# Weights behind the attention: split by two GpSimd loads instead of a load, a cast and a subtraction

## The chip, the cores and the metric

The kernel runs on one core of a Trainium2 chip. The metric is the device time of one execution in microseconds. The profile is of one execution, taken by the hardware profiler.

## The reference

One layer of a hybrid decoder block over 512 real positions and 16 leading meta positions, 1024 wide, all in fp32. Two attention branches of 16 heads each run side by side (MLA with rotary parts, and FoX with a cumulative forget gate), and their outputs are merged:

```python
u = rmsnorm(h, pre_norm_g)
proj = u @ w_in                        # q, k, v, z of both branches, gate_a, gate_b
...
y_mla = (o_mla * silu(z_mla)) @ w_br_mla
y_fox = (o_fox * silu(z_fox)) @ w_br_fox
mixed = (sigmoid(gate_a) * y_mla + sigmoid(gate_b) * y_fox) @ w_out
h = h + rmsnorm(mixed, post_norm_g)    # the meta positions are dropped at the end
```

## The kernel before

**Products in three passes.** TensorE multiplies a rounded fp32 type (`F32R`). To keep fp32 accuracy each operand is cut in a high half, its rounded value, and a low half, the rounded rest. A product is then three: high by high, high by low, low by high. A projection of 1024 inputs, 128 outputs and 512 positions is a *unit* of 8 x 3 = 24 products, accumulated in one bank of PSUM (three banks, pool `accp`). A unit's `done` takes the bank up.

**Weights.** `wload` asks SyncE's queue for a raw block of 128 x 1024 fp32 (512 KB, in rows of 512 bytes for `w_in` and the branch weights, of 2 KB for `w_out`). `wsplit` makes its halves: ScalarE casts raw to `wh` (L130), then `split_lo` (L103) subtracts, `wl = raw - wh`. The engine of the subtraction is `low[0]`: GpSimd up to the end of the attention, VectorE behind it. Raw blocks and both halves lie in the pool `wp`, three rooms of 4 KB per partition for each of `wraw`, `wh` and `wl`. A unit's halves are made when its first product is placed in the program, and `weights(...).load` lets the raw load be asked for up to three units ahead.

**What stands behind the attention.** The order of TensorE is written out by hand (`manual_schedule`); the other engines' orders, and those of the queues, are made by a scheduler from when things are ready and their priorities. The attention is filled up with projections, among them five gate units (`pg`); its last one, `tail`, surrounds the last product of the attention with its values (`ov`). Then the pools of the attention's inputs (`fctx`, `cctx`) are closed, and there follow:

- `halved_g(1)`, which cuts the FoX branch's output `gT[1]` into `gh` and `gl` (ScalarE and VectorE), and eight units `py(i, 1)` with `w_br_fox`, a gate unit behind each of the first three;
- `halved_g(0)`, four gate units, and eight units `py(i, 0)` with `w_br_mla`, a gate unit behind each of the first four;
- the product with `w_out` in a Strassen-like form of seven products of 24 each. Six of the fourteen weight blocks are loaded (`plain`, two 512-wide rows of `w_out` to a block), and eight are sums or differences that VectorE makes ahead of time in `tb` (`summed`);
- the second norm, the residual and the output.

That makes 11 gate units and 16 `py` units behind the attention, and 6 `plain` blocks. `gh` and `gl` lie in a pool `m2` of 16 KB each that opens behind the attention, and `yo` and `xr` (16 KB each) and `gp` (4 KB) in a pool `o1` that opens when `m2` is closed.

Of the kernel before, what the change touches and what calls it, by code (L numbers as in the profile page):

```python
# [12 lines left out]
F32R = mybir.dt.float32r  # L13
# [4 lines left out]
ALU = mybir.AluOpType  # L18
# [9 lines left out]
KD = D // 128  # L28
# [7 lines left out]
O_CQ, O_ZM, O_FQ, O_FK, O_FV, O_F, O_ZF, O_GA, O_GB = 0, 416, 1440, 2464, 3488, 4512, 4528, 5552, 6576  # L36
# [13 lines left out]
def f32(ap):  # L50
    return ap.bitcast(F32)
# [3 lines left out]
def block_kernel(ctx: ExitStack, tc: tile.TileContext, x, meta_tokens, pre_norm_g, w_in, fox_forget_b,  # L55
                 mla_q_norm_g, mla_kv_norm_g, w_uq, w_ukv, w_br_mla, w_br_fox, w_out, post_norm_g,
                 rope_tok, rope_pe, out):
    nc = tc.nc
    x2 = x[0]
    out2 = out[0]  # L60
    win = w_in[0].rearrange("(k p) f -> p k f", p=128)
    wout = w_out[0].rearrange("(k p) f -> p k f", p=128)
    wbr = [w_br_mla[0].rearrange("(k p) f -> p k f", p=128), w_br_fox[0].rearrange("(k p) f -> p k f", p=128)]
# [16 lines left out]
    c_dram = dram.tile([2, NH, L], F32, tag="cdram", name="c_dram")  # L80
    qpe_dram = dram.tile([NH, 2, 2, 16, S], F32, tag="qpedram", name="qpe_dram")

    wp = ctx.enter_context(tc.tile_pool(name="wp", bufs=3))
    uid = [0]
    written, sums_out = [False], []
    behind, through, first_t, exps, halved, lowered = [], [], [], [], {}, {}
# [1 line left out]
    def dma(out, src, start=None):  # L88

        with tc.issue_after(sums_out[1]) if written[0] and len(sums_out) == 2 else nullcontext():  # L90
            ins = (start or nc.sync.dma_start)(out=out, in_=src)
        if written[0]:
            tc.keep_in_program_order(ins)
        return ins.ins

    def mm(*a, **k):
        nc.tensor.matmul(*a, **k)  # L97
# [4 lines left out]
    def split_lo(eng, lo, src, hi):  # L102
        return eng.tensor_tensor(out=lo, in0=src, in1=f32(hi), op=ALU.subtract)  # L103

    def wload(srcs):

        uid[0] += 1
        u = uid[0]
        raw = wp.tile([128, 1024], F32, tag="wraw", name=f"wraw{u}")
        n = 0  # L110
        parts = []
        for src in srcs:
            dims = src.shape[1:]
            w = int(np.prod(dims))
            names = "abcd"[: len(dims)]
            pat = f"p ({' '.join(names)}) -> p {' '.join(names)}"
            rv = raw[:, n : n + w].rearrange(pat, **{c: d for c, d in zip(names, dims)})
            dma(rv, src)
            parts.append((n, w))
            n += w  # L120
        return u, raw, parts, n

    low = [nc.gpsimd]

    def wsplit(ld):

        u, raw, parts, n = ld
        wh, wl = (wp.tile([128, 1024], F32R, tag=t, name=f"{t}{u}") for t in ("wh", "wl"))
        with tc.issue_after(behind[0]) if behind else nullcontext():
            nc.scalar.copy(wh[:, :n], raw[:, :n])  # L130
        split_lo(low[0], wl[:, :n], raw[:, :n], wh[:, :n])
        return [(wh[:, o : o + w], wl[:, o : o + w]) for o, w in parts]

    def wunit(srcs):
        return wsplit(wload(srcs))

    def weights(srcs, wrap):

        st = {}

        def load():
            if "l" not in st:
                st["l"] = wload(srcs())

        def get():
            load()
            return wrap(wsplit(st["l"]))
        get.load = load
        return get

    def by_k(part, nk):

        h, l = (t.rearrange("p (k f) -> p k f", k=nk) for t in part)
        return (lambda k: h[:, k, :]), (lambda k: l[:, k, :])
# [15 lines left out]
    def acc(name):  # L170
        return accp.tile([128, 512], F32, tag="acc", name=name)
# [3 lines left out]
    def unit(name, getw, act, nk, sls, done):  # L175

        st = {}
        out = []

        def prep():  # L180
            if "w" not in st:
                st["w"] = getw()
            return True
        for i, sl in enumerate(sls):
            n = sl.stop - sl.start
            for k in range(nk):
                def fn(i=i, sl=sl, k=k, n=n):
                    if "b" not in st:
                        st["b"] = prep()
                        for load in getattr(out[0][1], "nxt", ()):  # L190
                            load()
                    if k == 0:
                        st["ps"] = acc(f"{name}{i}")
                    ps = st["ps"][:, :n]
                    (wh, wl), (ah, al) = st["w"], act(k)
                    for q, (w, a) in enumerate(((wh, ah), (wh, al), (wl, ah))):
                        mm(ps, w(k), a[:, sl], start=(k == 0 and q == 0), stop=(k == nk - 1 and q == 2))
                    if k == nk - 1:
                        done(i, ps)
                out.append((3 * n / 2.4, fn))  # L200
        out[0][1].prep = prep
        if hasattr(getw, "load"):
            out[0][1].load = getw.load
        return out

    REAL = [slice(META, L)]
# [11 lines left out]
    def win_w(off, i):  # L218
        return weights(lambda: [win[:, :, off + 128 * i : off + 128 * i + 128]], lambda w: by_k(w[0], KD))

    def run(steps):
        for _, fn in steps:
            fn()
# [322 lines left out]
    def gate_unit():  # L546

        i, br = gates.pop(0)

        def done(_, ps):  # L550
            ths[i, br] = thp.tile([128, S], F32, tag="th", name=f"th{i}{br}")
            nc.scalar.activation(ths[i, br], ps, AF.Tanh, scale=0.5)
        return unit(f"pg{i}{br}", win_w((O_GA, O_GB)[br], i), u_act, KD, REAL, done)


    with ExitStack() as att:
# [299 lines left out]
        def feed(br, pr):  # L856

            q = (q_mla, q_fox)[br](pr)
            k = (k_mla, k_fox)[br](pr)
            v, vts[br, pr] = v_unit(br, pr)  # L860
            return q, k, v
# [13 lines left out]
        for si, (br, pr) in enumerate(stages):  # L875
            last = si + 1 == len(stages)
            if not last:
                q, k, v = feed(*stages[si + 1])
# [87 lines left out]

    fctx.close()
    cctx.close()
    low[0] = nc.vector
    with ExitStack() as mg:  # L970
        mg.enter_context(tc.manual_schedule(engines={mybir.EngineType.PE}))
# [16 lines left out]

        def py(i, br):
            def get():  # L990
                return by_k(wunit([wbr[br][:, :, 128 * i : 128 * i + 128]])[0], KD)

            def done(_, ps):
                nc.vector.scalar_tensor_tensor(out=gT[br][:, i], in0=ths[i, br], scalar=1.0, in1=ps, op0=ALU.add, op1=ALU.mult)
            run(unit(f"py{i}{br}", get, lambda k: (gh[:, k, :], gl[:, k, :]), KD, [slice(0, S)], done))
            if br:
                return
            nc.vector.tensor_tensor(out=mx[:, i], in0=mx[:, i], in1=gT[1][:, i], op=ALU.add)
            src, (h, l) = (mx[:, i, 0:256], [t[:, i] for t in a1]) if i < HK else (mx[:, i], [t[:, i - HK] for t in a2])
            nc.scalar.copy(h, src)  # L1000
            split_lo(nc.vector, l, src, h)
# [20 lines left out]
        for i in range(KD):  # L1022
# [3 lines left out]
            if i == 2:  # L1026
                for n, (kb, c) in enumerate(((0, 0), (0, 1), (1, 1), (1, 0))):
                    for half in range(2):
                        k0 = HK * kb + 2 * half
# [7 lines left out]
        for n, i in enumerate(PAIRED):  # L1037
# [3 lines left out]
            elif n >= 4:  # L1041
                done = n // 2 if n < 7 else HK
# [18 lines left out]

        def plain(kb, n, c):
            k0 = HK * kb + 2 * c
            return by_k(wunit([wout[:, k0 : k0 + 2, 512 * n : 512 * n + 512]])[0], 2)

        def summed(n, c):
            uid[0] += 1
# [126 lines left out]
```

## Time and profile before

| | |
|---|---|
| time, median of 3 runs | 604.22 us (604.12 to 605.11) |
| the profiled execution | 603.71 us, of which the profile's span 601.8 us |
| TensorE products | 592.5 us busy, 98% of the span |
| VectorE, ScalarE, GpSimd | 62%, 57%, 30% busy |
| granted TensorE clock | 0.998 of full |
| last product of the attention | ends at 407.7 us |
| last gate of the attention | ends at 410.7 us |
| last `py` unit | ends at 557.6 us |
| last product | ends at 596.0 us |

A name like `wl<-wraw,wh` in a row of the profile is the tile written and the tiles read, without buffer numbers. `L103` is line 103 of the kernel. A row marked `SPq` is an issue of SyncE's DMA queue. Busy time of an engine says nothing on the end by itself; what counts is the chain of waits.

### The profile page before, as it was taken

The page shows a single profiled execution, that of the slowest core. Times are in us where ns is not written, and L with a number is a line of the kernel's source. Part 1 is how long each engine was busy: PE and PEld are TensorE (multiplying, and loading weights), DVE is VectorE, ACT ScalarE, POOL GpSimd, SP SyncE. Part 2 cuts the span into 40 slices and gives each one's busy share as a digit, 9 for nine tenths or more (in the row PEclk, how much of TensorE's full clock was granted, in tenths as well). Part 3 has the DMA queues.
Part 4 walks back from the last instruction along what each step waited for, and adds up shares of the span by engine and source line. Part 5 has one row for each costly group of instructions (what it writes and reads, how often), then busy time and mean ns, then how long its engine had stood idle before and what let it go on. Part 6 is the DMA issues. An engine that isn't in the chain of part 4 may idle for free.

```text
span 601.8 us, 10999 instructions
## 1 busy us (share of the span) xinstructions
PE 592.5 (98%) x3777; PEld 501.7 (83%) x3777; DVE 374.1 (62%) x1002; ACT 343.9 (57%) x788; POOL 180.6 (30%) x239
## 2 busy tenths in 40 slices
PE   8999999999999999999999999999999999999996
PEld 6889779789889889888898898888888888888884
DVE  4956776674675674766657747764733524367857
ACT  7847765774783784766747747851222423353653
POOL 4316635443348453443523534430000000000000
PEclk9999999999999999999999999999999999999999
DMA  8433699899796798988886875988533333332603
GB/s 294 107 84 86 134 196 208 193 189 231 96 185 152 171 200 178 189 191 170 163 158 154 201 160 140 193 163 281 182 97 105 106 86 89 105 104 91 228 0 141
DMA packets 219960, 93.25 MB, mean 155 GB/s; under 512 B 133420, under 2 KB 211636, under 8 KB 219904
## 3 DMA queue, kind: packets, MB, share of 16 engines
q1 hardware_dynamic: 219904, 92.55, 65.5%
q8 instruction: 30, 0.49, 0.3%
q14 instruction: 26, 0.21, 0.1%
HBM read 58.10 MB, written 4.00 MB: 103 GB/s over the span
## 4 chain that ended last, share of the span: by engine, by line
PE 92%; ACT 3%; DMA 2%; DVE 1%; issue 1%; POOL 1%; SPq 0%; DVEq 0%; ACTq 0%; POOLq 0%
PE z L97 16%; PE py L97 14%; PE pg L97 14%; PE v L97 9%; PE st L97 8%; PE fq L97 8%; PE fk L97 7%; PE ov L97 5%; PE x L97 4%; PE psm L97 2%; PE mq L97 2%; PE mk L97 1%; PE ppe L97 1%; DMA wsr<-in_w_in_dram 1%; PE y L97 1%; DMA ht<-in_x_dram 1%
## 5 line engine op out<-in xcount | busy, mean ns | idle before, releaser
L103 POOL TENSOR_TENSOR wl<-wraw,wh 128x1024 fp32r<-128x1024 f32 (+2 forms) x63 | 122.6, 1954 | 105.3 <-ACT wh L130 76.5
L130 ACT CAST wh<-wraw 128x1024 fp32r<-128x1024 f32 (+1 forms) x80 | 83.1, 1042 | 115.7 <-PE pg L97 38.6
L823 DVE SCALAR_TENSOR_TENSOR pn<-sf,ri,pn 128x128 f16<-128x128 f32 (+3 forms) x128 | 70.7, 592 | 13.9 <-ACT pn L822 13.8
L795 ACT ACTIVATE sf<-sf,nb 128x144 f32<-128x144 f32 (+3 forms) x128 | 72.0, 564 | 8.1 <-DVE nb L787 7.8
L822 ACT ACTIVATE pn<-sf,ri 128x128 f16<-128x128 f32 (+3 forms) x128 | 61.5, 551 | 20.4 <-ACT sf L795 17.6
L103 DVE TENSOR_TENSOR wl<-wraw,wh 128x1024 fp32r<-128x1024 f32 x33 | 40.3, 1223 | 42.4 <-ACT wh L130 42.4
L787 DVE CUSTOM_DVE_ANT_0 sf<-st,maskt 128x272 f32<-128x272 f32 (+2 forms) x128 | 48.6, 435 | 3.9 <-PE st L97 3.9
L97 PE MATMUL z<-uTh,wh 128*128 128x512 f32 x128 | 50.9, 398 | 0.0
L97 PE MATMUL z<-uTh,wl 128*128 128x512 f32 x128 | 50.1, 392 | 0.3 <-POOL wl L103 0.3
L97 PE MATMUL pg<-uTh,wh 128*128 128x512 f32 x128 | 50.3, 393 | 0.0
L97 PE MATMUL z<-uTl,wh 128*128 128x512 f32 x128 | 50.0, 391 | 0.0
L97 PE MATMUL pg<-uTl,wh 128*128 128x512 f32 x128 | 49.8, 389 | 0.0
L97 PE MATMUL pg<-uTh,wl 128*128 128x512 f32 x128 | 49.8, 389 | 0.0
L97 PE MATMUL py<-gh,wh 128*128 128x512 f32 x128 | 49.8, 389 | 0.0
L97 PE MATMUL py<-gl,wh 128*128 128x512 f32 x128 | 49.8, 389 | 0.0
L97 PE MATMUL py<-gh,wl 128*128 128x512 f32 x128 | 49.8, 389 | 0.0
L97 PE MATMUL st<-hlk,hlq 64*128 64x272 f32 (+3 forms) x480 | 47.3, 306 | 0.0
L97 PEld LDWEIGHTS st<-hlk,hlq 64*128 64x128 f32 x480 | 35.0, 185 | 5.8 <-ACT vh L719 2.8
L700 DVE TENSOR_REDUCE vsc<-v 128x1 f32<-128x272 f32 (+1 forms) x32 | 13.2, 432 | 37.9 <-PE v L97 37.9
L97 PE MATMUL v<-uTh,wl 128*128 128x256 f32 (+1 forms) x128 | 36.5, 285 | 0.0
L97 PE MATMUL fk<-uTl,wh 128*128 128x256 f32 (+1 forms) x128 | 36.4, 285 | 0.0
L97 PE MATMUL fk<-uTh,wh 128*128 128x256 f32 (+1 forms) x128 | 36.4, 285 | 0.0
(233 smaller groups left out, 1431.4 us busy)
## 6 DMA issues: line engine op xcount, KB each, us to landing
wraw<-in_w_in_dram SPq DMA_DIRECT2D x56, 512.0 KB, 4.1
wraw<-in_w_br_fox_dram SPq DMA_DIRECT2D x8, 512.0 KB, 3.6
tb<-in_w_out_dram SPq DMA_DIRECT2D x8, 512.0 KB, 7.4
wraw<-in_w_br_mla_dram SPq DMA_DIRECT2D x8, 512.0 KB, 3.6
wraw<-in_w_out_dram SPq DMA_DIRECT2D x6, 512.0 KB
pt<-pn SPq DMA_TRANSPOSE x128, 3.1
xr<-in_x_dram SPq DMA_DIRECT2D x4, 512.0 KB, 7.4
out_dram<-yo SPq DMA_DIRECT2D x8, 256.0 KB, 2.0
```

Source lines behind the costliest of these rows:

```text
L97: nc.tensor.matmul(*a, **k)
L103: return eng.tensor_tensor(out=lo, in0=src, in1=f32(hi), op=ALU.subtract)
L130: nc.scalar.copy(wh[:, :n], raw[:, :n])
L700: nc.vector.tensor_reduce(out=sc[:, i : i + 1], in_=ps, op=ALU.max, axis=AX.X, apply_absolute_value=True)
L787: nc.vector.tensor_tensor_reduce(out=sf_of(h, b)[:, c0 : c0 + w], in0=ps[h][:, o : o + w], in1=maskt[:, m0 : m0 + w], scale=-scale, scalar ...
L795: exps[g] = nc.scalar.activation(sf, sf, AF.Exp, bias=sums["nb"][:, h, b : b + 1], scale=-1.0, accum_out=sums["su"][:, h, b : b + 1]).ins
L822: nc.scalar.activation(hi, sf, AF.Copy, scale=rib)
L823: nc.vector.scalar_tensor_tensor(out=lo, in0=sf, scalar=rib, in1=hi, op0=ALU.mult, op1=ALU.subtract)
```

## The change

Behind the attention the pool `wp` is closed and a pool `wq` opened, with four rooms of 8 KB per partition, each for both halves of a block. A block's halves are made by a new function, `wdma`, without a raw copy on the chip: GpSimd issues a load that casts from fp32 to the rounded type on its way into `wh`; ScalarE writes `wl = -wh`; GpSimd issues the same load a second time, adding into `wl`. The 11 gate units built behind the attention, the 16 `py` units and the 6 `plain` blocks use it. The eight `summed` blocks keep the cast and the subtraction on VectorE, and take their halves' room from `wq`. The gate units inside the attention keep `win_w`.

```diff
-    wp = ctx.enter_context(tc.tile_pool(name="wp", bufs=3))
+    wctx = ExitStack()
+    wp = wctx.enter_context(tc.tile_pool(name="wp", bufs=3))
+    wq = []
...
     def wsplit(ld):
 
         u, raw, parts, n = ld
-        wh, wl = (wp.tile([128, 1024], F32R, tag=t, name=f"{t}{u}") for t in ("wh", "wl"))
+        if wq:
+            both = wq[0].tile([128, 2, 1024], F32R, tag="w", name=f"w{u}")
+            wh, wl = both[:, 0], both[:, 1]
+        else:
+            wh, wl = (wp.tile([128, 1024], F32R, tag=t, name=f"{t}{u}") for t in ("wh", "wl"))
...
-    def wunit(srcs):
-        return wsplit(wload(srcs))
+    def wdma(src):
+
+        uid[0] += 1
+        u = uid[0]
+        both = wq[0].tile([128, 2, 1024], F32R, tag="w", name=f"w{u}")
+        wh, wl = both[:, 0], both[:, 1]
+        rv = [w.rearrange("p (k f) -> p k f", k=src.shape[1]) for w in (wh, wl)]
+        nc.gpsimd.dma_start(out=rv[0], in_=src)
+        nc.scalar.mul(wl, f32(wh), -1.0)
+        nc.gpsimd.dma_start(out=rv[1], in_=src, accum_op=ALU.add)
+        return wh, wl
...
-        return unit(f"pg{i}{br}", win_w((O_GA, O_GB)[br], i), u_act, KD, REAL, done)
+        off = (O_GA, O_GB)[br] + 128 * i
+        get = win_w(off - 128 * i, i) if low[0] is nc.gpsimd else lambda: by_k(wdma(win[:, :, off : off + 128]), KD)
+        return unit(f"pg{i}{br}", get, u_act, KD, REAL, done)
...
     fctx.close()
     cctx.close()
+    wctx.close()
+    wq.append(ctx.enter_context(tc.tile_pool(name="wq", bufs=4)))
     low[0] = nc.vector
...
-                return by_k(wunit([wbr[br][:, :, 128 * i : 128 * i + 128]])[0], KD)
+                return by_k(wdma(wbr[br][:, :, 128 * i : 128 * i + 128]), KD)
...
-            return by_k(wunit([wout[:, k0 : k0 + 2, 512 * n : 512 * n + 512]])[0], 2)
+            return by_k(wdma(wout[:, k0 : k0 + 2, 512 * n : 512 * n + 512]), 2)
```

## The prediction

> **What bounds the kernel now.** I read the busy time of the engines first, then the stretches behind the attention, then the chain of waits there. The windows view gives per row: the stretch, its length, then busy time and instructions of PE, its weight loads, VectorE (DVE), ScalarE (ACT) and GpSimd (POOL), the granted TensorE clock, the DMA engines' busy share and GB/s.
>
> ```profile
> PE 592.5 (98%) x3777; PEld 501.7 (83%) x3777; DVE 374.1 (62%) x1002; ACT 343.9 (57%) x788; POOL 180.6 (30%) x239
> 443.00:470.00 27.00, 27.00 (x121) 22.37 (x120) 11.66 (x14) 9.51 (x13) 0.00 (x0) 1.00 0.35 95
> 470.00:557.00 87.00, 87.00 (x386) 72.06 (x385) 42.18 (x58) 30.45 (x44) 0.00 (x0) 1.00 0.33 96
> 557.00:596.00 39.00, 38.93 (x171) 31.61 (x169) 31.10 (x49) 23.22 (x41) 0.00 (x0) 1.00 0.30 112
> ```
>
> TensorE is busy in the whole of every stretch behind the attention, at the full clock; VectorE is busy half of the middle one, ScalarE a third, GpSimd not at all. Work taken off VectorE there cannot shorten anything. The chain of waits, in order of time (start, length, what), says the same:
>
> ```profile
> 407.74 2.95 PE pg L97 x12
> 410.69 5.44 PE py L97 x24
> 416.13 5.44 PE pg L97 x24
> 421.57 5.44 PE py L97 x24
> ...
> 535.81 21.76 PE py L97 x96
> 557.57 5.44 PE x L97 x24
> ...
> 590.23 5.73 PE x L97 x24
> ```
>
> Each of the 27 units `pg` (11) and `py` (16) is 24 products in 5.44 us, so 0.227 us a product, and the next begins in the moment the last one ends. There is no gap to close, so the change can gain nothing here; the question is only whether the weights still arrive in time.
>
> Who brings them now is seen in the issues of SyncE's queue (start, length, what) in the page's list of DMA issues, whose last number is the median from issue to landing, and in the tile view of the raw weights (ns: shortest/median/longest, then the first and last start):
>
> ```profile
> 382.28 0.37 SPq L91 DMA_DIRECT2D wraw<-in_w_br_fox_dram  x1
> 387.75 10.86 SPq L91 DMA_TRANSPOSE pt<-pn  x8
> 408.56 1.40 SPq L1030 DMA_DIRECT2D tb<-in_w_out_dram  x3
> wraw<-in_w_in_dram SPq DMA_DIRECT2D x56, 512.0 KB, 4.1
> wraw<-in_w_br_fox_dram SPq DMA_DIRECT2D x8, 512.0 KB, 3.6
> tb<-in_w_out_dram SPq DMA_DIRECT2D x8, 512.0 KB, 7.4
> L103 DVE TENSOR_TENSOR wl<-wraw,wh x33: 1212/1224/1227, 399.6 to 577.5; 128x1024 fp32r<-128x1024 f32 x33
> L130 ACT CAST wh<-wraw x80: 637/1053/1129, 24.0 to 576.4; 128x1024 fp32r<-128x1024 f32 x78, 128x512 fp32r<-128x512 f32 x2
> ```
>
> The first `py` unit starts at 410.69, and its raw weights were asked for at 382.28, 28 us ahead and in the middle of the attention. A load, a cast of 1.05 us and a subtraction of 1.22 us are hidden many times over.
>
> **The change part by part.**
>
> *Taken away, at no gain.* For the 33 units with weights of their own (11 gates, 16 `py`, 6 `plain`) 33 subtractions on VectorE go (33 x 1.224 = 40 us) and 33 loads leave SyncE's queue. ScalarE keeps 33 passes of the same size, a negation in place of the cast; I take 1.05 us. All of that lay under 100% TensorE, so its removal is worth nothing. Nothing of the 11 gates' work inside the attention changes: the units built there still take the old way.
>
> *The transition.* The new rooms take the place of the old weight pool, which is closed before them; everything below it on that side was closed too. What a new pool waits for is shown once, at the end of the `py` units, where `yo`, `xr` and `gp` go where `gh` and `gl` were (SyncE's queue, the waits there, and the last row of GpSimd):
>
> ```profile
> 557.60 0.34 SPq L1057 DMA_DIRECT2D gp<-in_post_norm_g_dram  x1
> SPq L1057 <- PE py L97: 2.9, 1, 2.9
> 395.13 2.79 POOL L103 TENSOR_TENSOR wl<-wraw,wh 128x1024 fp32r<-128x1024 f32 x1
> ```
>
> `gp` is declared behind `yo` and `xr`, which alone fill the 32 KB of `gh` and `gl`, and yet its load sits in SyncE's queue for 2.9 us until the last `py` product (535.81 + 21.76 = 557.57). So the first use of a pool waits for the last use of all that lay in the pool beneath. The last user of the old weight pool is the gate `pg` that ends at 407.74 + 2.95 = 410.69. Before that no room of the new pool may be filled; GpSimd, whose last own instruction starts at 395.13, waits there with 66 loads behind it, and TensorE, whose order is written out, has nothing else to do. The old pool is 9 rooms of 4 KB, the new one 4 of 8 KB; the halves `gh` and `gl`, which come next, so move onto the old pool's last 4 KB and wait for the same moment; their first piece takes one ScalarE and one VectorE pass of some 0.7 us and the rest keeps pace, so the weights cover it.
>
> TensorE then stands still for casting load, negation, adding load. Neither kind of load is in this trace. From below each is bounded by the fastest load of 512 KB, 3.6 us; from above I use 7.4 us, the landing of loads of that size that were issued in a burst (`tb`). For the casting load I take 4.1 us (`w_in`, the same size and 512-byte rows). For the adding one I take 7.4 us: four rooms are free at once, so it stands behind three more casting loads. 4.1 + 1.05 + 7.4 = 12.55 us (ends: 8.25 and 15.85).
>
> By the formula of the Trainium skill (DMA: Bandwidth & Descriptors, "Anatomy of one DMA"), 2.0 us plus the bytes at 436 GB/s, a load issued by GpSimd would take an estimated 3.2 us; the gap would then be 7.5 us, the pace of the later units 5.6 us, and the whole about 614 us, near my lower end. No run here has such a load yet.
>
> *The clock after that gap.* TensorE idles at the start and at the end of this run:
>
> ```profile
> 2.07 4.34 PE L97 MATMUL spun<-CT,ONE 128*128 128x512 f32 x10 [2.07 <-DVE ONE L236]
> 596.00:599.00 3.00, 0.00 (x0) 0.00 (x0) 2.83 (x5) 0.97 (x3) 0.00 (x0) 1.00 0.45 175
> 599.00:602.00 3.00, 0.00 (x0) 0.00 (x0) 0.00 (x0) 0.00 (x0) 0.00 (x0) 0.65 0.45 175
> ```
>
> After the last product at 596.0 the clock stays full for 3 us and averages 0.65 in the next 3; if it falls to half, that is at about 599.9, 3.9 us into the idle time. The first ten products of the run took 0.434 us each, against 0.227 later. A gap of 12.55 us is long enough, so I add 10 x (0.434 - 0.227) = 2.1 us once (ends: 0 and 2.1). The Trainium skill has this as a rule (TensorE: Matmul & The Clock Gate, "What's actually happening"): half clock after about 3.4 us without work, full clock again after about 3.4 us of work, which would make it about 1.7 us; the trace's last two stretches agree with the first half of it.
>
> *The pace afterwards.* Of a unit the adding load must wait for the negation, and that for the casting load; both loads are issued by GpSimd in order. Where the queue alternates, casting and adding load of one unit, then of the next, the next unit's casting load stands behind this unit's adding load. Then one unit costs the casting load's landing, the negation, and the issue of the adding load. The issue is bounded by the two kinds in SyncE's queue: 0.37 us for a plain load, 10.86 / 8 = 1.36 us for a transposing one. I take 1.36, since these requests are the harder kind. 4.1 + 1.05 + 1.36 = 6.51 us against 5.44: 1.07 us a unit (ends: 0, since 3.6 + 1.05 + 0.37 = 5.02 is below 5.44; and 7.4 + 1.05 + 1.36 - 5.44 = 4.37).
>
> Four units have rooms at once, 23 follow. Each of those has a lead of three units, 16.32 us, against a chain of 12.55, so 3.8 us are free before the loss is felt: 23 x 1.07 - 3.8 = 20.8 us. Why alternating is likelier than not: in the present kernel a room comes free only when TensorE is done with it, one each 5.44 us, and a load with its negation (5.15 us) is done before the next comes free.
>
> *The output product.* Its first four weights are used up in 2.72 us each, half a unit. The last of their rooms comes free as the last `py` ends, TensorE arrives 3 x 2.72 = 8.2 us later, and its chain takes at least 4.1 + 1.05 + 4.1 = 9.25: 1.1 us lost (ends: 0 and 7.7). The eight `summed` weights come from a buffer that is there and stay as they are.
>
> *Sum*, on the profiled execution's own 603.71 us: 603.7 + 12.55 + 2.1 + 20.8 + 1.1 = 640.2 us. The median of the runs lies 0.5 us above the profiled one, so 640.7. The lower ends give 603.7 + 8.25 = 612, the upper ones 603.7 + 15.85 + 2.1 + 100 + 7.7 = 729 (the 100 is 23 x 4.37 less the half microsecond that is left of the lead).
>
> **The rivals.**
>
> *The transition alone.* If the order of GpSimd's queue has the next unit's casting load ahead of this unit's adding load, two chains overlap, a chain of 12.55 us fits into the lead of 16.32, and only the first gap, the clock and the output product stay: 603.7 + 12.55 + 2.1 + 1.1 + 0.5 = 620. For it: the order of the queues follows when things are ready and not the text (the `py` load at 382.28 stands ahead of transposes of the attention). Against it: the 5.15 us above. Chance 0.25.
>
> *The DMA engines become the bound.* Now a unit's one load keeps them busy 0.33 of the time, 0.33 x 5.44 = 1.8 us. An adding load must also read what it adds to. At three times a plain load for both together they would be busy 5.4 of 5.44 us, which is just hidden; at four times for the adding load alone it is 5 x 1.8 = 9.0 us a unit, 23 x 3.56 = 82 us, and the whole 603.7 + 12.55 + 2.1 + 82 + 1.1 + 0.5 = 702. It decides from 5.44 us on. For it: an adding load has to fetch twice what a casting one does, and no row here bounds its price from above. Against it: none shows an addition to be slow either. The Trainium skill (Collectives: The Full Stack, "The bandwidth ceiling") holds that an adding transfer is slower for its two reads and not for the addition; by that rule the pace would stay at 5.4 us and this rival would fall. Chance 0.13.
>
> *Not slower.* If the new rooms wait only for the tiles that lay where they are, the first ones, over raw buffers that have long been read, can be filled in the attention. It decides at 410.69 - 12.55 = 398.1: a first casting load issued before that leaves no gap, and with a hidden pace the time is 604. It can end below that by no more than the few tenths of noise, as TensorE has no idle time to give. Against it stands the wait of `gp`. Chance 0.05 for no change and 0.02 for faster.
>
> That the casting load copies the bits and does not round would make the low halves zero, and change no time: the number of products is the same.
>
> **How the numbers follow.** The forecast, a gap and an alternating queue, has 0.55; the rivals have 0.25, 0.13, 0.05 and 0.02. The range 612 to 729 takes in the ends of the forecast's terms, the whole of the second case, and the lighter half of the third; about 0.8. A measurement of this kernel tells about 0.2%, 1.2 us, from no change. Slower by more than that: 0.55 + 0.25 + 0.13 and a little of the fourth case, 0.94; same 0.04; faster 0.02.
>
> **What the changed profile would show.** Right: a gap of TensorE from 410.7 on that ends with an adding load, of 8 to 16 us; a lower clock just behind it; from then on short gaps ahead of each `pg` and `py` unit, some 1 us, put down to a DMA; GpSimd's queue waiting for ScalarE's negation with a casting load behind it; VectorE 40 us less busy, everything ahead of 405 us as before. Wrong: a first casting load before 398 (no gap); units at 5.44 us back to back behind the gap (first rival); DMA engines at a share near 1, or GpSimd busy without a break while TensorE waits (the bound lies in the loads themselves, and the pace is far above 6.5 us).

## The result and the profile after

The change makes the kernel slower: 696.88 us median (693.49 to 697.26, four runs) against 604.66 us (604.12 to 605.55, four runs), a ratio of 1.151 with a 95% interval of 1.147 to 1.155. The profiled execution took 696.67 us, with a span of 694.9 us; before it was 603.71 and 601.8.

The page of the changed kernel: busy time of the engines, the granted clock and the DMA engines' share in 40 slices, the engines' shares in the chain that ended last, and the loads with the median from issue to landing:

```profile
PE 619.4 (89%) x3777; PEld 515.9 (74%) x3777; DVE 334.5 (48%) x969; ACT 342.9 (49%) x788; POOL 256.7 (37%) x305
PEclk9999999999999999999999995899998998988789
DMA  9524798998869899598877649999999989997453
PE 56%; issue 21%; DMA 8%; POOL 8%; ACT 4%; DVE 1%; SPq 0%; DVEq 0%; POOLq 0%; ACTq 0%
w<-in_w_in_dram POOLq DMA_DIRECT2D x22, 512.0 KB, 7.6
w<-in_w_br_fox_dram POOLq DMA_DIRECT2D x16, 512.0 KB, 7.7
...
w<-in_w_out_dram POOLq DMA_DIRECT2D x12, 512.0 KB, 7.2
```

TensorE does the same 3777 products, but it carries 56% of the chain where it carried 92%. VectorE lost 39.6 us of work and the end of the kernel did not feel it. The clock, at full speed throughout before, falls in the 25th slice (417 to 434 us), just behind the attention, and shows less than nine tenths in seven of the fifteen slices after that. The new loads take 7.2 to 7.7 us to land, in the median of both kinds together.

Where the time went is seen in the windows behind the attention (columns as in the prediction):

```profile
412.60:442.00 29.40, 8.65 (x24) 6.47 (x25) 14.26 (x16) 8.94 (x13) 10.08 (x8) 0.59 1.32 277
442.00:500.00 58.00, 49.84 (x207) 39.92 (x206) 4.13 (x6) 8.77 (x10) 18.18 (x15) 0.95 0.91 137
500.00:560.00 60.00, 50.77 (x197) 39.95 (x196) 8.00 (x13) 14.95 (x22) 19.78 (x16) 0.90 0.98 142
560.00:628.00 68.00, 56.39 (x217) 44.76 (x217) 17.89 (x30) 18.98 (x29) 21.56 (x18) 0.87 0.89 139
628.00:670.00 42.00, 27.65 (x109) 21.50 (x108) 16.62 (x27) 17.34 (x28) 8.92 (x9) 0.86 0.69 169
```

TensorE's idle time is the length of a row less its busy time: 20.75 us in the first, then 8.16, 9.23 and 11.61, and 14.35 in the stretch of the output product. Of the 29.0 us in the three middle rows, 27 are seven waits of 2.5 to 5.2 us each, and not a short one ahead of each unit. Set against the profile before, the span of 694.9 us is made up as follows. All values are in us.

| part | before | after | more | forecast |
|---|---|---|---|---|
| to the end of the last gate | 410.7 | 412.5 | 1.9 | 0 |
| first gap | 0 | 20.8 | 20.8 | 12.55 |
| the other `pg` and `py` units: idle | 0 | 29.0 | 29.0 | } 20.8 pace |
| the same: slower products | 146.9 | 167.6 | 20.7 | } and 2.1 clock |
| output product | 38.4 | 59.0 | 20.5 | 1.1 |
| behind the last product | 5.8 | 6.0 | 0.2 | 0 |

The gate's end, the end of the last `py` unit at 629.9 and that of the last product at 688.9 are read from TensorE's timeline; 167.6 is what is left of 412.5 to 629.9 without the idle time.

The first gap, from the timelines of TensorE, GpSimd, ScalarE and SyncE's queue (start, length, what, and in brackets the idle time ahead with what ended it; L147 is the casting load, L148 the negation, L149 the adding load):

```profile
412.15 0.39 PE L99 MATMUL pg<-uTh,wl 128*128 128x512 f32 x1
410.48 4.32 SPq L1049 DMA_DIRECT2D tb<-in_w_out_dram  x8
413.20 1.14 POOL L147 DMA_DIRECT2D w<-in_w_br_fox_dram  x1 [15.35 <-PE pg L99]
426.83 1.06 ACT L148 ACTIVATE w<-w 128x1024 fp32r<-128x1024 f32 x1 [9.52 <-DMA w<-in_w_br_fox_dram]
428.19 1.58 POOL L149 DMA_DIRECT2D w<-in_w_br_fox_dram  x1 [11.21 <-ACT w L148]
434.54 1.19 PE L99 MATMUL py<-gh,w 128*128 128x512 f32 x2 [6.41 <-DMA w<-in_w_br_fox_dram]
```

The first casting load is issued just behind the last product of the last gate, as forecast. But it needs 13.6 us to land (413.20 to 426.83) among eight loads `tb`, 4 MB, that are issued from 410.48 on; without them it takes 4.6 us (the run without `tb`, below). The negation is as forecast, and the adding load takes 6.4 us, from 428.19 to the next product at 434.54.

Then the steady part of GpSimd's queue:

```profile
539.28 1.54 POOL L149 DMA_DIRECT2D w<-in_w_in_dram  x1 [8.31 <-ACT w L148]
540.17 1.55 POOL L147 DMA_DIRECT2D w<-in_w_br_mla_dram  x1
541.06 1.56 POOL L147 DMA_DIRECT2D w<-in_w_in_dram  x1
548.64 1.57 POOL L149 DMA_DIRECT2D w<-in_w_br_mla_dram  x1 [6.02 <-ACT w L148]
550.08 1.73 POOL L149 DMA_DIRECT2D w<-in_w_in_dram  x1
550.98 1.73 POOL L147 DMA_DIRECT2D w<-in_w_br_mla_dram  x1
561.09 1.54 POOL L149 DMA_DIRECT2D w<-in_w_br_mla_dram  x1 [8.38 <-ACT w L148]
...
615.77 1.58 POOL L149 DMA_DIRECT2D w<-in_w_br_mla_dram  x1 [6.38 <-ACT a1h L1019]
```

It goes mostly in turns: "add, cast, cast", then "add, add, cast". At the head of each turn stands an adding load that waits for a negation, and that negation waits for a casting load that was issued behind the adding load of the turn before. Two turns bring three units in 561.09 - 539.28 = 21.81 us, so 7.27 us a unit, where TensorE needs 5.44. Over all 27 units, from the first adding load at 428.19 to the last for a `py` unit at 615.77, it is 187.6 / 26 = 7.21 us. Three of the longer waits behind 395 us (total us, times, longest); the first row is the largest of all, an adding load that waits for a negation:

```profile
POOL w L149 <- ACT w L148: 117.0, 18, 11.2
ACT w L148 <- DMA w<-in_w_br_fox_dram: 43.8, 6, 14.3
PE py L99 <- DMA w<-in_w_br_fox_dram: 28.9, 4, 14.4
```

In the output product the longest wait, 8.18 us, is for an adding load that leaves at 639.72. Its casting load had been issued at 628.84 and needed 9.2 us to land. Beside it SyncE's queue asks for the four blocks `xr`, 2 MB:

```profile
630.51 2.11 SPq L1078 DMA_DIRECT2D xr<-in_x_dram  x4
647.04 1.19 PE L99 MATMUL y<-w,a2h 128*128 128x512 f32 x2 [8.18 <-DMA w<-in_w_out_dram]
```

The next casting load, issued at 630.41, takes 11.7 us; the last two of the kernel, issued at 657.47 and 660.20 with neither `xr` nor an adding load right ahead of them, take 4.1 and 4.0.

### The profile page after: what moved, and what is told of

Its sections match the earlier page's. It is cut to its first block, busy times and chain, and to the rows that moved or that the text cites. A ratio compares the mean times of both kernels' runs of the same rounds, so it can differ in the third digit from the quotient of the medians.

```text
span 694.9 us, 11041 instructions
## 1 busy us (share of the span) xinstructions
PE 619.4 (89%) x3777; PEld 515.9 (74%) x3777; DVE 334.5 (48%) x969; ACT 342.9 (49%) x788; POOL 256.7 (37%) x305
## 4 chain that ended last, share of the span: by engine, by line
PE 56%; issue 21%; DMA 8%; POOL 8%; ACT 4%; DVE 1%; SPq 0%; DVEq 0%; POOLq 0%; ACTq 0%
PE z L99 13%; PE v L99 8%; PE st L99 7%; PE fk L99 7%; PE fq L99 6%; PE ov L99 5%; POOL w L149 4%; DMA w<-in_w_br_fox_dram 4%; PE pg L99 4%; POOL w L147 3%; DMA w<-in_w_out_dram 3%; PE psm L99 2%; PE x L99 2%; PE mq L99 1%; DMA pt<-pn 1%
## 5 line engine op out<-in xcount | busy, mean ns | idle before, releaser
L99 PE MATMUL py<-gh,w 128*128 128x512 f32 x256 | 90.1, 430 | 39.0 <-DMA w<-in_w_br_fox_dram 28.9
L148 ACT ACTIVATE w<-w 128x1024 fp32r<-128x1024 f32 x33 | 35.0, 1059 | 169.9 <-issue 59.9
L99 PEld LDWEIGHTS py<-gh,w 128*128 128x128 f32 x256 | 53.1, 210 | 54.5 <-issue 30.3
L840 DVE SCALAR_TENSOR_TENSOR pn<-sf,ri,pn 128x128 f16<-128x128 f32 (+3 forms) x128 | 70.5, 590 | 14.6 <-ACT pn L839 14.6
L99 PE MATMUL pg<-uTh,w 128*128 128x512 f32 x176 | 59.9, 416 | 10.8 <-DMA w<-in_w_in_dram 10.8
L1013 DVE SCALAR_TENSOR_TENSOR gT<-th,py 128x512 f32<-128x512 f32 x16 | 11.0, 686 | 114.8 <-PE py L99 88.8
L136 ACT CAST wh<-wraw 128x1024 fp32r<-128x1024 f32 (+1 forms) x47 | 48.5, 1035 | 14.5 <-PE v L99 11.7
L99 PE MATMUL py<-gl,w 128*128 128x512 f32 x128 | 54.4, 425 | 0.0
L99 PEld LDWEIGHTS pg<-uTh,w 128*128 128x128 f32 x176 | 35.0, 202 | 20.4 <-issue 10.9
L826 POOL TENSOR_TENSOR mt<-sf,ri 128x96 f32<-128x96 f32 (+1 forms) x32 | 9.4, 295 | 79.5 <-DVE ri L821 63.7
L149 POOL DMA_DIRECT2D w<-in_w_in_dram x11 | 17.5, 1593 | 55.6 <-ACT w L148 47.0
```

The source lines that it names most:

```text
L148: nc.scalar.mul(wl, f32(wh), -1.0)
L149: nc.gpsimd.dma_start(out=rv[1], in_=src, accum_op=ALU.add)
L826: nc.gpsimd.tensor_tensor(out=mt, in0=src, in1=ri.unsqueeze(3).broadcast_to([128, 2, nb_, META]), op=ALU.mult)
L840: nc.vector.scalar_tensor_tensor(out=lo, in0=sf, scalar=rib, in1=hi, op0=ALU.mult, op1=ALU.subtract)
```

## The experiments

Two theories stood at the start. In the one called Q, the pace comes from GpSimd's queue working in order: a chain of dependent loads that the order lets run one after the other. In the one called E, it comes from the time of the loads in the DMA engines, whose share of 0.89 to 0.98 in the table of windows looks like a bound. Each ratio is to the kernel before in the same group of runs. That took 604.42 us beside the first four kernels below; 604.43 beside the order of the queue, the idle products with nothing pinned, the waits tile by tile and the adding loads alone; and 605.36 beside the other four.

**The new pool without the new loads.** The rooms of `wq` stay, but SyncE loads a raw block and ScalarE and VectorE split it as before.

```diff
-        nc.gpsimd.dma_start(out=rv[0], in_=src)
-        nc.scalar.mul(wl, f32(wh), -1.0)
-        nc.gpsimd.dma_start(out=rv[1], in_=src, accum_op=ALU.add)
...
+        nc.sync.dma_start(out=raw.rearrange(...), in_=src)
+        nc.scalar.copy(wh, raw)
+        split_lo(nc.vector, wl, raw, wh)
...
-    wq.append(ctx.enter_context(tc.tile_pool(name="wq", bufs=4)))
+    wq.append(ctx.enter_context(tc.tile_pool(name="wq", bufs=3)))   # raw, wh and wl
```

> The change without its GpSimd loads: the pool is closed and a new one opened as in the change, but a unit's weights come by one plain load of SyncE's queue, a ScalarE cast and a VectorE subtraction, in three rooms each. It leaves only the price of the new pool. Recorded theory of the gap (the new pool waits for the last gate): TensorE stands still once, from 410.7 on, for a load, a cast and a subtraction, 4.1 + 1.05 + 1.22 = 6.4 us, up to some 16 us where the load stands among the 4 MB of `tb` loads (the first load of the change took 13.6 us), then a lower clock for about 2 us and no gap: 613 to 623 us. Rival (the rooms could be filled early): 604 to 606.

It took 614.02 us (612.98 to 617.87), ratio 1.018 (1.014 to 1.021). SyncE's queue and TensorE in the timeline:

```profile
410.40 0.37 SPq L148 DMA_DIRECT2D r<-in_w_br_fox_dram  x1
417.27 0.80 PE L99 MATMUL py<-gh,w 128*128 128x512 f32 x1 [6.96 <-ACT w L149]
```

The window:

```profile
442.00:500.00 58.00, 58.00 (x258) 48.02 (x257) 22.24 (x25) 18.55 (x24) 0.00 (x0) 1.00 0.33 93
```

The gate ends at 410.31 and the first load into the new rooms leaves at 410.40, where before the same weights were asked for at 382.28. TensorE stands still once, for 6.96 us, and never again before the output product. So the closing of the old pool alone opens the gap, whoever loads. It costs some 10 us of the 92: the gap, and 2.9 us by which the `pg` and `py` units take longer behind it (149.8 us against 146.9).

**No adding load.** The low halves stay the negated high halves.

```diff
-        nc.gpsimd.dma_start(out=rv[1], in_=src, accum_op=ALU.add)
```

> Leaves out the adding load: the low half stays minus the high half. One casting load and one negation a unit. Theory E (the DMA engines are the bound; the two loads of a unit hold them some 7 us, of which the casting one 2.8): 2.8 is far below 5.44, so only the first gap and its clock are left, 620 to 632 us. Theory Q (order of the queue and waits for the negation): no load waits for a negation any more, same forecast. It sizes the casting load and what the adding load costs: 65 to 75 us of the 92.

It took 625.19 us (624.2 to 626.49), ratio 1.035 (1.032 to 1.038). From its page:

```profile
w<-in_w_in_dram POOLq DMA_DIRECT2D x11, 512.0 KB, 4.0
w<-in_w_br_fox_dram POOLq DMA_DIRECT2D x8, 512.0 KB, 4.4
```

A window:

```profile
442.00:500.00 58.00, 58.00 (x258) 48.02 (x257) 10.13 (x15) 17.66 (x22) 8.83 (x11) 1.00 0.54 99
```

A casting load among casting loads lands in 4.0 to 4.4 us; my 4.1 was right for it, and only for it. The units follow one another at 5.44 us. The first gap is 14.6 us, of the casting loads and `tb` together. In the output product 2.4 us are lost, behind the one casting load that is issued beside `xr` (576.09) and lands in 10.0 us where the three before it took 4.0 to 4.1. The rest of the 92 us, some 71, is there only when there are adding loads.

**The adding load made a second casting load.** Same queue, same waits, same bytes written.

```diff
-        nc.gpsimd.dma_start(out=rv[1], in_=src, accum_op=ALU.add)
+        nc.gpsimd.dma_start(out=rv[1], in_=src)
```

> The second load casts like the first and does not add (the low half becomes the high half again): same instructions, order, waits and bytes from memory, only nothing is read back and added. Theory E: 2 x 2.8 = 5.6 us of the DMA engines a unit, just over 5.44: 635 to 650 us. Theory Q (order and waits): the second load still waits for the negation, with the same queue behind it; near the change's 697, at least 680 us.

It took 651.96 us (650.91 to 653.0), ratio 1.079 (1.077 to 1.082): 2 us above what theory E gave and 28 us below what theory Q gave, so it decided nothing by itself. Its loads land in 5.1 to 5.6 us (`w_in` and the branch weights), the window from 442 to 500 has no idle time and that from 500 to 560 has 4.1 us. Either theory can make that of a lighter second load: less time in the engines, or a shorter chain.

**Wider rows.** All loads of `wdma` fetch other data, blocks of `w_out` whose rows have 2 KB.

```diff
+        k0, f0 = 2 * (u % 4), 512 * (u // 4 % 2)
+        src = wout[:, k0 : k0 + 2, f0 : f0 + 512]
```

> Loads other data: every unit's 512 KB comes out of the output weights in rows of 2 KB in place of 512 bytes, cast and added as in the change, same bytes, same order and waits. Theory E: in the change's trace a 2 KB packet holds an engine some 98 ns for a casting and 176 ns for an adding load, against 42 and 64 ns for 512 bytes, so a unit needs 16 x 0.274 = 4.4 us in place of 7: below 5.44, only the first gap and the output product's waits stay, 622 to 640 us. Theory Q: order and waits are as they were, 680 us or more.

It took 689.99 us (688.25 to 698.49), ratio 1.145 (1.137 to 1.152), the same within the intervals as the change itself. A window:

```profile
442.00:500.00 58.00, 50.60 (x205) 40.94 (x205) 3.44 (x5) 9.92 (x11) 15.47 (x16) 0.91 0.62 136
```

The loads on its page:

```profile
w<-in_w_out_dram POOLq DMA_DIRECT2D x66, 512.0 KB, 7.5
```

The DMA share fell from 0.91 to 0.62 and neither the landing (7.5 us) nor TensorE's idle time (7.4 us in this window against 8.16) followed. The share is not what holds the loads up. That speaks against E, though not to the end, since the bytes are the same.

**Only the order of the queue.** The same loads into the same rooms with the same arithmetic; the casting load of the next unit (`wcast(n + 1)`) is put ahead of this unit's adding load by hand, for all but the last two blocks of `w_out`.

```diff
+        if n + 1 < len(wseq) - 2:
+            wcast(n + 1)
...
         nc.scalar.mul(wl, f32(wh), -1.0)
-        nc.gpsimd.dma_start(out=rv[1], in_=src, accum_op=ALU.add)
+        with tc.issue_after(last):
+            ahead_of["add"] = nc.gpsimd.dma_start(out=lo, in_=wseq[n], accum_op=ALU.add).ins
```

> The change with only the order of GpSimd's queue set by hand: the casting load of the next unit always ahead of the adding load of this one, so that its negation can be made while the adding load is under way. Same loads, bytes, rooms. Theory Q: the pace falls from 7.3 to between 5.44 and 6 us a unit, and the slow clock behind the gaps goes with the gaps; the first gap and the output product's stay: 630 to 655 us. Theory E: nothing changes, 690 to 700 us.

It took 653.78 us (652.61 to 657.75), ratio 1.082 (1.077 to 1.087). Two windows:

```profile
442.00:500.00 58.00, 58.00 (x257) 48.03 (x256) 9.99 (x16) 16.20 (x21) 26.98 (x22) 1.00 1.28 187
500.00:560.00 60.00, 60.00 (x266) 49.70 (x265) 7.99 (x13) 17.00 (x22) 26.30 (x22) 1.00 1.34 196
```

A load in GpSimd's queue:

```profile
508.40 0.90 POOL L149 DMA_DIRECT2D w<-in_w_in_dram  x1 [3.21 <-PE pg L99]
```

This decides between the two. The same loads go through the same engines at one unit in 5.44 us, with TensorE busy all the time. The queue now waits mainly for TensorE to free a room (`<-PE pg`) and hardly for the negation. The DMA share is higher than in the change, 1.28 and 1.34 against 0.91 and 0.98: it counts packets that overlap, and 0.91 to 0.98 was far from full. Theory E falls for the pace. The order alone is worth about 42 us (1.151 less 1.082, times 604.5). Left over are the first gap (14.5 and 6.7 us) and 17.2 us of idle time in the output product.

**The strict alternation.** GpSimd's queue is written out: four casting and four adding loads, then c4 a4 c5 a5 and so on to the end, which is the order that my prediction assumed.

```diff
+    turns = ("c0 c1 c2 c3 a0 a1 a2 a3 c4 a4 c5 a5 c6 a6 ... c32 a32").split()
...
+        with tc.issue_after(ahead_of["last"]) if "last" in ahead_of else nullcontext():
```

> The change with the order of GpSimd's queue pinned to strict alternation (four casting and four adding loads, then casting, adding of one unit after the other), which is the order that the run with idle products had, without the idle products. If that run's 753 us came from its order: 742 to 756 us, a unit each 9.3 us. If its idle products cost their 37 us: 712 to 720 us.

It took 758.82 us (758.05 to 762.39), ratio 1.256 (1.252 to 1.260), 3 us above the upper end of what was expected from the order. GpSimd's queue (L156 casts, L161 adds):

```profile
504.72 1.56 POOL L161 DMA_DIRECT2D w<-in_w_br_fox_dram  x1 [7.23 <-ACT w L160]
505.61 1.59 POOL L156 DMA_DIRECT2D w<-in_w_in_dram  x1
514.32 1.54 POOL L161 DMA_DIRECT2D w<-in_w_in_dram  x1 [7.12 <-ACT gh L1025]
542.73 1.54 POOL L161 DMA_DIRECT2D w<-in_w_in_dram  x1 [7.14 <-ACT w L160]
```

From one adding load to the next it takes (542.73 - 504.72) / 4 = 9.5 us. The 24 casting loads that stand behind an adding one here landed in (us, shortest, median, longest):

```profile
DMA to landing us min/median/max: 6.8/7.2/7.6
```

The parts of the 9.5 us are thus 0.9 from the adding to the casting load in the queue, 7.2 for the landing, 1.06 for the negation, and some 0.4 in which one engine hands over to the next. Most of the 7.2 us is the adding load ahead. In all runs the loads of GpSimd's queue landed in the order in which they were issued: the adding load of 504.72 landed at 511.1, 6.4 us after its issue, and the casting load of 505.61 at 512.6, 1.5 us behind it. One set of loads thus has three paces by order alone: 5.44 us a unit at most, 7.27 and 9.5.

An earlier kernel, **six idle products in front of each unit** and nothing pinned, was to test the clock. With the new products the scheduler chose this alternation, so the kernel tested the order instead of the clock.

```diff
+                        for _ in range(6 if fillp else 0):
+                            mm(fillp[0], uTh[:, 0, 0:128], uTh[:, 0, META:L], start=True, stop=True)
```

> The change with six idle products (on data that is there, into a bank of their own) ahead of each of the 27 gate and py units behind the attention: 6 x 0.227 = 1.36 us a unit. Where the queue sets a pace of 7.3 us, TensorE has 1.8 us a unit to spare, so they cost nothing. If the slow clock behind the gaps is felt in the end (some 21 us of lost product time up to the last py unit), keeping TensorE at work saves part of it: 675 to 690 us. If the clock is absorbed by the wait for the queue: 694 to 702 us. If the pace were TensorE's own: 27 x 1.36 = 37 us more, 730 us.

It took 753.03 us (751.15 to 755.41), ratio 1.245 (1.240 to 1.250). That is outside all three values expected. It says nothing on the clock, and agrees with the run above on the order.

**The clock with the order held.** GpSimd's queue is that of the change, written out, with the same six idle products a unit.

```diff
+    turns = ("c0 c1 c2 c3 a0 a1 a2 a3 c4 a4 c5 a5 c6 c7 a6 a7 c8 a8 c9 c10 ... a31 a32").split()
...
+                        for _ in range(6 if fillp else 0):
+                            mm(fillp[0], uTh[:, 0, 0:128], uTh[:, 0, META:L], start=True, stop=True)
```

> The six idle products ahead of each of the 27 units again, now with GpSimd's queue pinned to the change's own order. Slow clock absorbed (the queue sets the pace, TensorE's slower products fall into time in which it would wait): 692 to 702 us. Slow clock felt: 675 to 690 us. Idle products paid for (TensorE sets the pace): 710 to 735 us.

It took 705.33 us (703.56 to 707.08), ratio 1.166 (1.163 to 1.168), 8 us above the change: between what was expected of an absorbed clock and of idle products that cost time. A window:

```profile
442.00:500.00 58.00, 57.37 (x253) 47.10 (x252) 4.13 (x6) 8.99 (x10) 18.15 (x15) 1.00 0.83 124
```

The adding load of the last `py` unit in GpSimd's timeline:

```profile
617.78 1.58 POOL L161 DMA_DIRECT2D w<-in_w_br_mla_dram  x1 [6.36 <-ACT a1h L1043]
```

The clock is full here and in the next window, up to 560 us, where the change had 0.95 and 0.90, and the kernel is no faster. The last adding load for a `py` unit leaves at 617.78, where it was 615.77: GpSimd's queue keeps its own time whether TensorE runs fast or slow. So the slower products in the `pg` and `py` units were not what made the time; at the full clock TensorE waits longer for the same weights. The idle products, 27 x 6 x 0.227 = 36.8 us of work at the full clock, fell mostly into those waits. Ahead of the last units they made waits of their own, of 4.76 and 3.83 us, for the tile `uTh` that they read and that ScalarE was rewriting, so the 8 us need not be a price of the clock. What the slow clock costs in the first gap and the output product is not separated by this.

**The first gap without `tb`.** Order as in the change, written out; the eight loads of `tb` are held back until the third `py` unit is done, by one element of its result that is written into `tb` first.

```diff
+                        nc.vector.tensor_copy(tb[n][0:1, 2 * half, 0:1], gT[1][0:1, 2, 0:1])
                         nc.sync.dma_start(tb[n][:, 2 * half : 2 * half + 2], wout[...])
```

> The change with its queue order pinned, and the 4 MB of tb loads made to wait for the third py unit (one element of tb written from its result first), so that they no longer stand beside the first four casting loads. If they are why the first of these took 13.6 us to land, TensorE's first gap falls from 20.8 us to 12 to 15: 686 to 692 us. If not: 694 to 699 us.

It took 696.11 us (693.99 to 697.64), ratio 1.150 (1.147 to 1.153): no difference in sum, which by the total is what was expected if `tb` were not the cause. Its timeline shows two differences that cancel:

```profile
417.99 1.58 POOL L161 DMA_DIRECT2D w<-in_w_br_fox_dram  x1 [2.23 <-ACT w L160]
456.04 4.33 SPq L1093 DMA_DIRECT2D tb<-in_w_out_dram  x8
473.42 1.22 PE L99 MATMUL py<-gh,w 128*128 128x512 f32 x2 [12.01 <-DMA w<-in_w_br_fox_dram]
```

The first adding load leaves at 417.99 where it was 428.19, and the first gap falls from 20.8 to 5.4 + 7.4 = 12.8 us. So `tb` made the difference there. The loads of `tb`, now issued at 456, hold up the chain of weights at that place: TensorE waits 12.0 us where it waited 4.2 in the change.

**The old pool waited for tile by tile.** The new rooms wait only for the tiles that lay in their place.

```diff
-    wq.append(ctx.enter_context(tc.tile_pool(name="wq", bufs=4)))
+    wq.append(ctx.enter_context(tc.tile_pool(name="wq", bufs=4, reuse_waits="tile")))
-        m2 = mgg.enter_context(tc.tile_pool(name="m2", bufs=1))
+        m2 = mgg.enter_context(tc.tile_pool(name="m2", bufs=1, reuse_waits="tile"))
```

> The change with the new weight pool and the pool of gh and gl told to wait tile by tile for what lay where their rooms are, and not for the last use of the whole pool beneath. Recorded theory of the gap: the first room lies over raw blocks that have been read by some 398 us, so its casting load goes out about then and most of the 20.8 us that TensorE loses behind the last gate (14.4 and 6.4) go: 675 to 686 us. Rival (the gap comes from the loads, not from the wait): 692 to 698 us.

It took 693.84 us (690.77 to 699.98), ratio 1.148 (1.142 to 1.155): missed. GpSimd's and ScalarE's timelines:

```profile
398.62 1.14 POOL L147 DMA_DIRECT2D w<-in_w_br_fox_dram  x1 [0.32 <-POOL wl L105]
413.53 4.25 ACT L1005 CAST gh<-gT 128x512 fp32r<-128x512 f32 x8
417.68 2.00 ACT L148 ACTIVATE w<-w 128x1024 fp32r<-128x1024 f32 x2
419.03 1.58 POOL L149 DMA_DIRECT2D w<-in_w_br_fox_dram  x1 [4.22 <-ACT w L148]
```

The first casting load does leave at 398.62, inside the attention, and its data are there at 405.3, well before the gate ends at 413.0. But the negation stands on ScalarE behind the eight casts of `gh`, and these behind the last gate's own `th`; the adding load stands behind the casting loads of two rooms that are not free, and needs 13.6 us to land, behind those two loads and among `tb`. TensorE waits 1.2 and 17.4 us. The wait moved from the pool to the order of two queues and to the burst of `tb`. The same **with the order of the queue mended too**:

> The casting load one unit ahead (the order of the run with 654 us) together with tile-by-tile waits, so that neither the queue's order nor the old pool holds the first unit: its casting load at 398, its adding load some 7 us later, the weights there at about 412. If the first gap is the old pool's wait and the queue's order together, nearly all of its 21 us and their slow clock go: 628 to 640 us, what is left lying in the output product. If the loads themselves hold it: 648 to 656 us.

Its four executions took 643.11, 645.73, 649.49 and 654.16 us; the ratio, 1.068 (1.063 to 1.073), is that of the first three. That is some 8 us below the order alone (1.082 less 1.068, times 605) and missed the 628 to 640 us expected, for the same reason. The profiled execution is that of 654.16 us, which was late already in the attention; only the order of its rows is used:

```profile
417.04 4.25 ACT L1022 CAST gh<-gT 128x512 fp32r<-128x512 f32 x8
422.55 1.58 POOL L166 DMA_DIRECT2D w<-in_w_br_fox_dram  x1 [12.47 <-ACT w L164]
```

**Only the adding loads on GpSimd.** SyncE brings a raw block, ScalarE casts and negates.

```diff
-        nc.gpsimd.dma_start(out=rv[0], in_=src)
+        nc.sync.dma_start(out=raw.rearrange(...), in_=src)
+        nc.scalar.copy(wh, raw)
...
```

> The casting load is replaced by a plain load of SyncE's queue into one raw room, a ScalarE cast and the negation; the adding load stays on GpSimd, whose queue now holds adding loads alone. Theory Q (each adding load waits for a negation with casting loads behind it, and the landing of these stands behind the last adding load): that circle is gone, the units run at 5.44 us, the first gap and its clock stay: 620 to 632 us. Theory E (the DMA engines' time): 1.8 + 4.2 = 6.0 us a unit by the packets' durations: 635 to 650 us.

It took 644.5 us (642.93 to 647.5), ratio 1.067 (1.062 to 1.072). By the total alone that would have gone to theory E, but the window shows the pace of Q:

```profile
442.00:500.00 58.00, 58.00 (x258) 48.02 (x257) 9.22 (x16) 27.68 (x33) 16.88 (x11) 1.00 1.12 192
```

With the other load in another queue, nothing that an adding load waits for stands behind an adding load of GpSimd's, and the units run at 5.44 us. The excess is in the first gap (8.5 and 10.7 us) and the output product (some 11 us).

No version was faster than the kernel before. Behind its attention TensorE has no idle time that one of them could win.

## Why the prediction was right and wrong

**Right:** the bound (TensorE full, nothing to gain), the direction, and the gap's start. The first room is filled only when the last user of the old pool is done (413.20 against 412.54, and 410.40 against 410.31 with SyncE's loads). Right too was the mechanism of the pace: a chain of casting load, negation and adding load that GpSimd's order forces into single file, shown by the kernel that changes the order alone and by the strict alternation. The measured time lies inside the range; the forecast's total was 56 us too low, in three terms that go back to one step: the casting load's landing was taken as 4.1 us wherever the load stands.

**The pace, forecast 6.51 us a unit, measured 7.27.** The failing step is the casting load's landing, taken as 4.1 us from a plain load of the same rows. Among other casting loads it is 4.0 to 4.4. Behind an adding load, where the alternating order always puts it, it is 7.2 (6.8 to 7.6), since it lands only behind that load. I applied that thought to the adding load in the first gap and not to the casting load in the steady part. The issue was taken as 1.36 us and is 0.9, which is small beside that, and the some 0.4 us of handing over had no term. In the order that I assumed the pace would have been 9.5 us. That 7.27 is nearer to my 6.51 is luck: the scheduler took turns that are milder than the strict alternation, and this error took back part of the other. With this landing nearly all of the lead of three units is gone too: in the change the casting loads from 448 us on land in 8.2 us in the median, and 8.2 + 1.06 + 6.6 = 15.9 us of the 16.32 are used up. So 26 x (7.21 - 5.44) = 46 us come from the pace, where I had 20.8; the `pg` and `py` part behind the first gap lost 49.7 in all.

**The first gap, forecast 12.55, measured 20.8.** The adding load (6.4 against 7.4) and the negation were well sized. The casting load was not: 13.6 us instead of 4.1. The eight `tb` loads had landed in 7.4 us in the profile before, and I used that row as a price for the adding load and did not see that `tb`, whose issue at 408.56 stands in the prediction's own rows, would be under way beside the first casting load. Without it the gap is 12.8 us.

**The output product, forecast 1.1, measured 20.5.** The place was right, the price came from the same 4.1 us. Weights there are used up in 2.72 us each against 7.27 in which they arrive. 14.35 us of idle time follow, and some 6 us of slower products. With the order mended 17.2 us of idle time are still there, so the queue's order alone is not their cause. An adding load that is issued beside `xr` there, at 585.17, needs 13.5 us to land, and TensorE waits 8.4 us for it, which looks like the same mistake as with `tb`. No run holds `xr` back, so its share is not shown.

**The clock, forecast 2.1 us once.** It falls again behind many of the later gaps (0.95, 0.90, 0.87 in the windows), which makes 20.7 us of slower products. Yet with the order held and the clock full up to 560 us nothing was won in the `pg` and `py` part, which waits for weights in either case. The forecast's 2.1 us, added to the pace as a cost of its own, belonged at most to the first unit.

**The rivals.** That the DMA engines become the bound gave 702 us, close to the time measured, and a DMA share of 0.9 to 0.98, which I had named as its sign, was there. Both were chance: with a higher share, 1.34, the same loads keep 5.44 us a unit. In the change's trace a packet of 512 bytes takes some 42 ns casting and 64 ns adding, 1.5 times as long. A unit of 2 x 1024 packets on 16 engines would by that hold each of them for 64 x (42 + 64) ns = 6.8 us, more than 5.44; but packets overlap, and with the order mended the same ones fit. What the engines need can be estimated from loads that stand one behind another: in the first gap the casting ones land 1.5 us apart (428.6, 430.0, 431.5) and the adding ones 2.9 (437.6, 440.6, 443.5), an estimated 4.4 us a unit, below 5.44. The Trainium skill (Collectives: The Full Stack, "The bandwidth ceiling") lays the cost of an adding transfer on its two reads; the packets, 1.5 times a casting one's, agree in kind, and by that rule the rival falls, as it did.

"The transition alone" (620 us) has the order of the kernel that changes the order alone; that gave 654. Of the 34 us between, 8.6 are the longer first gap and 16 the idle time of the output product; the rest is about what the slower products cost (TensorE is busy for 603.1 us, 10.6 more than before, of which 2.1 were forecast). By the Trainium skill (DMA: Bandwidth & Descriptors, "Anatomy of one DMA") a load would take an estimated 3.2 us, and the kernel 614; the runs show 4.0 to 4.4 for a casting load among its like and 7.2 to 7.7 in the changed kernel, so here the formula holds for neither.

**Open.** The attention ends 1.9 us later in the profile after; in the other kernels that leave its loads alone its last gate ends anywhere from 410.3 to 412.2, and the cause is not found. A version that mends the pool's wait and ScalarE's order together was not tried, and neither was one that holds `xr` back.

## What to carry to other kernels

When a step is cut into loads that depend on each other and one in-order queue issues them, price the first load of a unit as it stands in the queue, behind the second load of the unit before, and not alone; and write the order out: the next unit's first load ahead of this unit's second. A load that seems hidden in a steady part shows its whole chain wherever the pool changes, the units get shorter, or another burst starts at the same moment. A busy share of the DMA engines near 1 is no proof of a bound; change the order or the row length at the same bytes and see whether the time follows.

## What the runs showed of the hardware

- The DMA share of the windows counts overlapping packets and goes to 1.34 in a stretch in which TensorE never waits; at 0.98 in the change there was room for a third more loads in the same time (5.44 us a unit against 7.27).
- An adding load of 512 KB in rows of 512 bytes takes GpSimd 1.5 to 1.6 us to issue where its queue holds adding loads alone, a casting one 0.88 us where it holds casting loads alone. A casting load right behind an adding one still starts 0.9 us after it.
- The loads of GpSimd's queue landed in the order of their issue in every run here.
- A casting load lands in 4.0 to 4.4 us (medians by source) among casting loads and in 6.8 to 7.6 us behind an adding one in the strict alternation, 1.5 us behind that load, and rows of 2 KB instead of 512 bytes do not change the landing of the mixed loads (7.5 us against 7.2 to 7.7).
